# Head pairs 0 and 1 of a hybrid attention layer: attention weights as two 16-bit parts, turned by transposing transfers

## The chip, the cores and the metric

The kernel runs on one core of a Trainium2 chip. A core has TensorE (matrix products, results only into PSUM), VectorE (called DVE in the profile), ScalarE (ACT), GpSimd (POOL) and SyncE (SP, whose queue issues most transfers). Each engine works through its own queue in order; semaphores make one wait for another. The metric is the time of one launch in microseconds of device time. Three runs of the kernel before took 662.28, 662.69 and 664.75 us, so its median is 662.69 us.

## The reference

One layer on a sequence of 1024 positions, width 1024, all in float32:

```python
mod = silu(c) @ w_ada + b_ada                      # shift, scale, gate
u   = layer_norm(x) * (1 + scale) + shift
h   = u @ w_in                                     # q, k, v, g of both groups, and 8 forget gates
# stick-breaking heads (8):
z = q k^T / 8;  w = exp(log_sigmoid(z) + later)    # later: sum of log_sigmoid(-z) over the keys between
# forgetting heads (8):
p = softmax(q k^T / 8 + f_q - f_k), causal
y = concat(heads * silu(g)) @ w_out
out = layer_norm(2**0.25 * x + gate * y) * ln_g + ln_b
```

Heads are 64 wide. Two heads make a pair: pairs 0 to 3 are the stick-breaking heads, pairs 4 to 7 the forgetting ones. The change is in pairs 0 and 1.

## The kernel before

**Precision.** A float32 product is made of three products of rounded parts: both operands are split into a rounded part and a rest (`u_hi`, `u_lo`; `whi`, `wlo`), and hi x hi, lo x hi and hi x lo are added in PSUM (`m_step`, L329 to L331).

**Order.** The order of TensorE's instructions is written out by hand; the order on the other engines is made by a scheduler from the same text, and so is SP's after the start. In the first 80 us the input is normalised and turned (`u_turn`, `u_round`, `u_rest`), the first five projections are made (`start_steps`), and the value tiles of pairs 0 and 1 (`v_first`). Then come 128 units, one for a pair, a head and a block of 128 queries: `u = (p, h, i)`, `order(p)` gives their order. Around each unit TensorE gets a share of the remaining projections as filler (`fillers`, `FILL`: 52 steps around pair 0, 72 around pair 1, 68 around pairs 2 and 3). At the end comes the output projection (`o_step`, L1112 to L1114).

**A unit of pairs 0 to 3.** `att_scores` makes the scores in a PSUM tile S (L611, L613), ACT makes two sigmoids (`kp` at L646, `be` at L648), DVE a running product (L654, L658), POOL multiplies (L660): `be` now holds the unit's weights, 128 queries by (i+1) * 128 keys.

**From weights to output, pairs 0 and 1.** `att_transpose`, two units later (`LAG`), has TensorE turn each 128 x 128 block of `be` into a PSUM tile T (L691; two such tiles); ACT rounds it into `pt` (L693) and DVE subtracts for the rest (L694). Two units make a block of 256 queries; `att_pv` then multiplies both parts with the values in one 512-column product for each 128 keys (L720), and `att_sum` adds three pieces (L738 to L740), multiplies by the gate (L741) and stores.

**Pairs 2 and 3 (and 4 to 7) instead.** ACT writes `be` times 2**15 as float16 (L671), DVE the rest as float16 (L673), and SP issues a transposing transfer that turns both parts inside the SBUF tile called `home` (L572). `att_pv` comes five units later (`LAG_CROSSED`) and makes two float16 products of 256 columns for each 128 keys (L709). Values too are two float16 parts, scaled by a factor that `gen_ranges` finds beside the units of pair 0: sums of squares of the value weights (L396), the largest modulation (L386, L388), and from them a power (L408 to L422). `FIRST_CROSSED` is the first pair that goes this way.

PSUM is full: while T tiles are needed, S has one buffer; later the two banks of T become a second S.

## Time and profile before

| | |
|---|---|
| median of three runs | 662.69 us |
| the profiled execution | 664.71 us, its span 663.0 us |
| TensorE busy | 635.6 us (96%), weight loads 535.5 us |
| DVE, ACT, POOL busy | 511.8, 397.8, 344.3 us |
| first 80.2 us | projections and values of the start |
| pair 0, pair 1 (first to first weights) | 80.2 to 149.7, 149.7 to 223.6 us |
| pair 2, pair 3 | 223.6 to 287.9, 287.9 to about 345 us |

A line of the profile names the source line, the engine, the operation, output <- input, and the shape as partitions x elements; times are from the start of the span. A matmul's duration is from its start until its result is out, and neighbours overlap: what one adds to TensorE's queue is the distance from start to start. The stage boundaries are the starts of the first L648 of each pair.

### The profile page before, as it was taken

The page shows a single profiled execution, that of the slowest core. Times are in us where ns is not written, and L with a number is a line of the kernel's source. Part 1 is how long each engine was busy: PE and PEld are TensorE (multiplying, and loading weights), DVE is VectorE, ACT ScalarE, POOL GpSimd, SP SyncE. Part 2 cuts the span into 40 slices and gives each one's busy share as a digit, 9 for nine tenths or more (in the row PEclk, how much of TensorE's full clock was granted, in tenths as well). Part 3 has the DMA queues.
Part 4 walks back from the last instruction along what each step waited for, and adds up shares of the span by engine and source line. Part 5 has one row for each costly group of instructions (what it writes and reads, how often), then busy time and mean ns, then how long its engine had stood idle before and what let it go on. Part 6 is the DMA issues. An engine that isn't in the chain of part 4 may idle for free. (4 is left out here: it accounts for less than half of the span.)

```text
span 663.0 us, 10902 instructions
## 1 busy us (share of the span) xinstructions
PE 635.6 (96%) x3558; PEld 535.5 (81%) x3558; DVE 511.8 (77%) x1011; ACT 397.8 (60%) x833; POOL 344.3 (52%) x429
## 2 busy tenths in 40 slices
...
GB/s 319 402 312 135 167 123 110 104 58 28 58 33 10 71 115 112 160 118 157 106 172 153 174 139 153 139 147 125 115 198 137 245 284 176 205 232 129 94 33 63
DMA packets 153800, 96.25 MB, mean 145 GB/s; under 512 B 118224, under 2 KB 133136, under 8 KB 153744
## 3 DMA queue, kind: packets, MB, share of 16 engines
...
q14 instruction: 28, 0.23, 0.1%
...
## 5 line engine op out<-in xcount | busy, mean ns | idle before, releaser
L329 PE MATMUL m<-uh,whi 128*128 128x512 f32 x304 | 123.0, 405 | 1.2 <-DVE kl L316 1.2
L331 PE MATMUL m<-uh,wlo 128*128 128x512 f32 x304 | 119.8, 394 | 0.0
L330 PE MATMUL m<-ul,whi 128*128 128x512 f32 x304 | 119.8, 394 | 0.0
L660 POOL TENSOR_TENSOR be<-be,kp 128x127 f32<-128x127 f32 (+3 forms) x64 | 89.9, 1405 | 44.9 <-DVE kp L658 24.2
L741 POOL TENSOR_TENSOR ty<-ty,sg 64x256 f32<-64x256 f32 x64 | 49.8, 779 | 91.6 <-DVE ty L736 56.0
L654 DVE TENSOR_TENSOR_SCAN kp<-kp,floor 128x128 f32<-128x128 f32 (+3 forms) x64 | 58.5, 914 | 14.8 <-ACT kp L646 14.1
L611 PE MATMUL S<-k,q 128*128 128x512 f32 (+4 forms) x192 | 68.5, 358 | 1.0 <-ACT be L648 1.0
L331 PEld LDWEIGHTS m<-uh,wlo 128*128 128x128 f32 x304 | 57.2, 188 | 13.6
L329 PEld LDWEIGHTS m<-uh,whi 128*128 128x128 f32 x304 | 57.4, 189 | 12.0 <-PE m L331 1.2
L613 PE MATMUL S<-kl,qz 128*128 128x512 f32 (+4 forms) x192 | 65.8, 344 | 0.0
L330 PEld LDWEIGHTS m<-ul,whi 128*128 128x128 f32 x304 | 57.4, 189 | 9.7
L622 DVE CUSTOM_DVE_ANT_0 a<-S,fb 128x1024 f32<-128x1024 f32 (+7 forms) x64 | 48.2, 753 | 19.7 <-PE S L613 15.8
L628 ACT ACTIVATE a<-a,nm 128x1024 f32<-128x1024 f32 (+7 forms) x64 | 49.7, 776 | 19.8 <-DVE nm L622 18.9
L638 DVE SCALAR_TENSOR_TENSOR home<-a,l,home 128x1024 f16<-128x1024 f32 (+7 forms) x64 | 58.1, 907 | 3.5 <-ACT home L634 3.3
L634 ACT ACTIVATE home<-a,l 128x1024 f16<-128x1024 f32 (+7 forms) x64 | 49.3, 773 | 16.2 <-DVE l L630 9.0
L646 ACT ACTIVATE kp<-S 128x384 f32<-128x384 f32 (+4 forms) x96 | 43.7, 491 | 23.7 <-PE S L613 21.9
L709 PE MATMUL pv<-home,v_g 128*128 128x256 f16 x480 | 56.3, 265 | 0.7 <-DVE ty L736 0.7
L709 PEld LDWEIGHTS <-v_g 128*128 128x128 f16 x480 | 44.2, 99 | 15.1 <-issue 9.8
L441 PE MATMUL v<-whi_v,uh 128*128 128x256 f32 (+1 forms) x192 | 54.7, 285 | 0.0
L443 PE MATMUL v<-wlo_v,uh 128*128 128x256 f32 (+1 forms) x192 | 54.4, 283 | 0.0
L442 PE MATMUL v<-whi_v,ul 128*128 128x256 f32 (+1 forms) x192 | 54.1, 282 | 0.0
L1112 PE MATMUL o<-woh,whi_y 128*128 128x512 f32 (+1 forms) x119 | 47.4, 398 | 5.4 <-DVE sg L322 4.8
...
## 6 DMA issues: line engine op xcount, KB each, us to landing
...
```

The source lines that it names most:

```text
L329: nc.tensor.matmul(acc, hi[:, c], u_hi[kt][:, s], start=(kt == 0), stop=False)
L330: nc.tensor.matmul(acc, hi[:, c], u_lo[kt][:, s], start=False, stop=False)
L331: nc.tensor.matmul(acc, lo[:, c], u_hi[kt][:, s], start=False, stop=(kt == NB - 1))
L441: nc.tensor.matmul(acc[:, :n], u_hi[kt][:, ts_], hi[:, s], start=(kt == 0), stop=False)
L442: nc.tensor.matmul(acc[:, :n], u_lo[kt][:, ts_], hi[:, s], start=False, stop=False)
L443: nc.tensor.matmul(acc[:, :n], u_hi[kt][:, ts_], lo[:, s], start=False, stop=(kt == NB - 1))
L611: nc.tensor.matmul(S[:, s, :w], qst[p][h][:, qs], kst[p][h][:, ks], start=True, stop=False)
L613: nc.tensor.matmul(S[:, s, :w], z, klo[p][:, ks], start=False, stop=not masked)
L638: lows[:] = [nc.vector.scalar_tensor_tensor(lo, ab, l, hi, op0=ALU.mult, op1=ALU.subtract)]
L654: last_dve = nc.vector.tensor_tensor_scan(rv, rv, floor[:, :ke - lo], initial=0.0, op0=ALU.mult, op1=ALU.max)
L660: nc.gpsimd.tensor_tensor(be[:, :ke - 1], be[:, :ke - 1], kp[:, 1:ke], op=ALU.mult)
L709: nc.tensor.matmul(acc[:, q0:256], vt[p][:, kb, h * P:(h + 1) * P], pt[:, 2 * kb + x_, q0:], start=(kb == 0 and x_ == 0), stop=(kb == last ...
```

## The change

`FIRST_CROSSED` goes from 2 to 0: pairs 0 and 1 go the way of pairs 2 and 3. T tiles, L691, L693, L694 and L720 are gone; S has two buffers from the first unit on. The values of pairs 0 and 1 are stored as float16 parts as they are made (`v_first`, in the start), so their factor is needed there: `range_sums`, four squares, `range_top`, `range_inverse` and `range_scales` stand in the last rounds of `start_steps`. `gen_ranges` keeps the factors of groups 1 to 3. The gate's last step (`gen_gate`) moves from beside pair 0 to beside pair 4. The order of units in pairs 0 to 3 is another, and the places in `home` for pair 0 are given by `FIRST_HOMES`.

```diff
@@ -25,7 +25,7 @@
 MASKED = -1.0e30
 BIG = 3.0e38
 UP = 2.0 ** 15
-FIRST_CROSSED = 2
+FIRST_CROSSED = 0
 
 
 @with_exitstack
...
@@ -376,16 +375,47 @@
 
     v_up, v_down, v_two = {}, {}, {}
 
+    rng = bss_sb.rearrange("p k i -> p (k i)")[:, 4:]
+
+    def range_sums():
+        nc.gpsimd.tensor_copy(modc[:, 1, :], bss_sb[:, 1, :])
+        m2 = bss_sb[:, 0, :]
+        nc.vector.tensor_reduce(out=m2, in_=modc.rearrange("p k i -> p i k"), op=ALU.max,
+                                axis=mybir.AxisListType.X, apply_absolute_value=True)
+        return nc.vector.tensor_tensor(rng[:, 0:1], m2[:, 0:1], m2[:, 1:2], op=ALU.add)
+
+    def range_top(row):
+        nc.tensor.transpose(row, rng[:, 0:1], ident)
+        return nc.vector.tensor_reduce(out=rng[0:1, 1:2], in_=row, op=ALU.max, axis=mybir.AxisListType.X)
+
+    def range_inverse(top_ps):
+        nc.tensor.matmul(top_ps, ones[0:1, :].to_broadcast([1, P]), rng[0:1, 1:2], start=True, stop=True)
+        top = rng[:, 2:3]
+        nc.vector.tensor_scalar(top, top_ps, 1.0e-30, None, op0=ALU.max)
+        nc.vector.reciprocal(top, top)
+
+    def range_scales(norm_ps, fr, g0, n):
+        nc.tensor.matmul(norm_ps, ones.to_broadcast([P, P]), fr, start=True, stop=True)
+        up, down = rng[:, 3 + g0:3 + g0 + n], rng[:, 7 + g0:7 + g0 + n]
+        nc.vector.tensor_reduce(out=up, in_=norm_ps.rearrange("p (g h) -> p g h", h=4), op=ALU.add,
+                                axis=mybir.AxisListType.X)
+        nc.vector.tensor_scalar(up, up, 1.0e-30, None, op0=ALU.max)
+        nc.gpsimd.tensor_tensor(up, up, mhalf.to_broadcast([P, n]), op=ALU.pow)
+        nc.gpsimd.tensor_scalar(up, up, rng[:, 2:3], 900.0, op0=ALU.mult, op1=ALU.mult)
+        nc.vector.reciprocal(down, up)
+        nc.vector.tensor_scalar(down, down, 1.0 / UP, None, op0=ALU.mult)
+        for g in range(n):
+            v_up[g0 + g], v_down[g0 + g] = up[:, g:g + 1], down[:, g:g + 1]
+
+    def square(out, w, at):
+        return nc.vector.tensor_tensor_reduce(out=out, in0=w, in1=w, op0=ALU.mult, op1=ALU.add, scale=1.0,
+                                              scalar=0.0, accum_out=at)
+
     def gen_ranges():
 
 
         for _ in range(NORM_AT):
             yield
-        nc.gpsimd.tensor_copy(modc[:, 1, :], bss_sb[:, 1, :])
...
@@ -393,35 +423,10 @@
                 raw = raw_tile(f"n{g}_{h}")[:, :n]
                 nc.sync.dma_start(raw, w_vf[h] if g == 1 else w_v[g - 1, h])
                 at = 4 * g - 4 + h
-                nc.vector.tensor_tensor_reduce(out=raw, in0=raw, in1=raw, op0=ALU.mult, op1=ALU.add, scale=1.0,
-                                               scalar=0.0, accum_out=fr[:, at:at + 1])
+                square(raw, raw, fr[:, at:at + 1])
                 for _ in range(NORM_SPACE):
                     yield
...
+        range_scales(s_tile("ranges", 2)[:, 0, :12], fr, 1, 3)
...
@@ -447,10 +452,11 @@
             v5 = v_two[g][:, :, t].rearrange("p i (x c) -> p i x c", c=HD)
             a5 = acc[:, :256].rearrange("p (i x c) -> p i x c", i=2, c=HD)
             up = v_up[g][:, 0:1]
-            nc.scalar.activation(v5[:, :, 0::3, :], a5, AF.Copy, scale=up)
+            upper = nc.scalar.activation(v5[:, :, 0::3, :], a5, AF.Copy, scale=up)
             for i in range(2):
-                nc.vector.scalar_tensor_tensor(v5[:, i, 1:3, :], a5[:, i], up, v5[:, i, 0::3, :],
-                                               op0=ALU.mult, op1=ALU.subtract)
+                v_evacs.append(upper)
+                v_evacs.append(nc.vector.scalar_tensor_tensor(v5[:, i, 1:3, :], a5[:, i], up, v5[:, i, 0::3, :],
+                                                              op0=ALU.mult, op1=ALU.subtract))
         for i in range(0 if g in v_two else 2):
             v4 = vt[2 * g + i].rearrange("p t (x c) -> p t x c", c=HD)
             a4 = acc[:, i * P:(i + 1) * P].rearrange("p (x c) -> p x c", c=HD)
...
@@ -540,6 +546,7 @@
     homes, parts_at = {}, []
 
     HOMES = ((1, 12), (2, 0), (1, 0), (0, 0))
+    FIRST_HOMES = ((2, 0), (0, 8), (0, 0), (2, 8), (1, 0), (0, 0), (2, 0), (1, 0))
     LAST_HOMES = ((2, 0), (2, 4), (4, 0), (4, 8), (0, 0), (1, 0), (4, 0), (0, 0))
 
     def home(n):
...
@@ -560,14 +567,14 @@
 
     def two_parts(u):
 
-        two = place(parts_at, ((3, 0, 16), (2, 8, 16)), u[2] + 1)
+        two = place(parts_at, ((3, 0, 16), (2, 8, 16)) if k_of[u] > 19 else ((3, 0, 16),), u[2] + 1)
         return two.rearrange("p b (x c) -> p b x c", x=2)
 
     def cross(u, two):
         p, h, i = u
         j, qo = i // 2, (i % 2) * P
         if (p, h, j) not in st_pt:
-            m, a = (LAST_HOMES if p == NPAIR - 1 else HOMES)[j if p < NPAIR - 1 else 2 * j + h]
+            m, a = FIRST_HOMES[2 * j + h] if p == 0 else LAST_HOMES[2 * j + h] if p == NPAIR - 1 else HOMES[j]
             st_pt[p, h, j] = home(m)[:, a:a + 4 * j + 4, :]
         sent[:] = [nc.sync.dma_start(st_pt[p, h, j][:, :2 * i + 2, qo:qo + P],
                                      two.rearrange("p b x c -> p (b x c)"), transpose=True)]
...
@@ -604,7 +611,7 @@
         qs = slice(i * P, i * P + P)
         if p >= 4:
             f = fb[2 * (p - 4) + h]
-        S = s_tile(f"S_{p}_{h}_{i}", 1 if k_of[u] < 16 * FIRST_CROSSED + LAG else 2)
+        S = s_tile(f"S_{p}_{h}_{i}", 2)
         halves = range(ns) if p >= 4 else range(ns)[::-1]
         for s in halves:
             ks = slice(s * w, s * w + w)
...
@@ -883,9 +890,12 @@
         last = kb == NB - 1
         if last:
             start_steps(ALL[:2], acc0, kb)
+            range_top(xt_early[0:1, :P])
             for n in range(2):
                 evac_m(*START[n], 0, acc0[n])
             start_steps(ALL[2:], acc0, kb)
+            range_inverse(xt_early[:, P:P + 1])
+            range_scales(xt_early[:, 2 * P:2 * P + 4], cm[:, :4], 0, 1)
             break
         start_steps(ALL[:4], acc0, kb, parts=(0,))
         if kb == 0:
...
@@ -941,6 +951,11 @@
             with after(rest, aggr[0]):
                 norm_stats(6)
             make_v(0)
+            with after(rest):
+                range_sums()
+                for n in range(4):
+                    square(v_two[0].rearrange("p i t c -> p (i t c)").bitcast(BF16)[:, :512],
+                           v0_raw[n], cm[:, n:n + 1])
 
     wg = {}
 
...
@@ -970,15 +981,16 @@
             parts.append((hi, lo))
             for _ in range(4):
                 yield
+        b = att_tile("bg")
+        nc.sync.dma_start(b, b_gate.to_broadcast([P, D]))
+        for _ in range(8):
+            yield
+        gp = s_tile("gate_ps", 2)
         for h in range(2):
             s = slice(h * 512, h * 512 + 512)
-            gp = t_tile(f"gate_{h}")
-
             for i, part in enumerate(parts[h]):
-                nc.tensor.matmul(gp, half.to_broadcast([P, P]), part, start=(i == 0), stop=(i == 1))
-            nc.vector.scalar_tensor_tensor(gate[:, s], b[:, s], 0.5, gp, op0=ALU.mult, op1=ALU.add)
-            yield
-            yield
+                nc.tensor.matmul(gp[:, h, :], half.to_broadcast([P, P]), part, start=(i == 0), stop=(i == 1))
+            nc.vector.scalar_tensor_tensor(gate[:, s], b[:, s], 0.5, gp[:, h, :], op0=ALU.mult, op1=ALU.add)
 
     def late_round(kb):
         u_turn(kb, 512, 1024)
...
@@ -1207,11 +1219,12 @@
 
     fillers = chain([
         beside(chain([gen_rest(), gen_v(0, v0_w, range(4, NB)), gen_m(1, 2), gen_m(2, 0), gen_m(2, 1)]),
-               gen_gate(), gen_ranges()),
+               gen_ranges()),
         gen_v(1),
         beside(chain([gen_m(2, 2), gen_m(3, 0), gen_m(3, 1), gen_m(3, 2)]), gen_forget()),
         gen_m(4, 0), gen_m(4, 1), gen_v(2),
-        gen_m(4, 2), gen_m(5, 0), gen_m(5, 1), gen_m(5, 2),
+        beside(chain([gen_m(4, 2), gen_m(5, 0)]), gen_gate()),
+         gen_m(5, 1), gen_m(5, 2),
         gen_m(6, 0), gen_m(6, 1), gen_v(3), gen_m(6, 2), gen_m(7, 0), gen_m(7, 1),
         gen_last_g(7),
     ])
...
@@ -1223,7 +1236,7 @@
     OUT0 = 5
     TAIL = (2, 2, 2, 2, 2, 2, 4, 4, 4, 4, 8)
     G7 = 6
-    HELD = {4: (1, 1), 5: (0, 0), 6: (1, 0), 10: (0, 1)}
+    HELD = {4: (1, 1), 5: (0, 0), 6: (1, 0), 8: (0, 1)}
     FIRST_UNITS = 5
     LNLOAD = 7
     YFIRST = 4
...
@@ -1231,17 +1244,16 @@
     done = [0]
 
     def fill(want):
-        while done[0] < want:
+        while done[0] < want - 1.0e-6:
             done[0] += 1
             next(fillers, None)
 
     def order(p):
         if p == 0:
-            return [(p, h, i + d) for i in (0, 4) for h in range(2) for d in range(4)]
-        if p < FIRST_CROSSED:
-            return [(p, h, i) for h in range(2) for i in range(NB)]
+            return [(p, h, i + d) for h in range(2) for i in (0, 2) for d in range(2)] + [
+                (p, h, i + d) for i in (4, 6) for h in range(2) for d in range(2)]
         if p < 4:
-            return [(p, h, i + d) for h in range(2) for i in (6, 4, 2, 0) for d in range(2)]
+            return [(p, h, i + d) for h in range(2) for i in (6, 2, 4, 0) for d in range(2)]
         if p < NPAIR - 1:
             return [(p, h, i) for h in range(2) for i in reversed(range(NB))]
         return [(p, h, i + d) for i in (2, 0, 4, 6) for h in range(2) for d in range(2)]
```

What the scheduler makes of it is shown at three places. The first is TensorE at the end of the first projections, where `ul_141` is the last block of the input's rest. Before:

```order
L826 MATMUL st_g_152<-ul_141,hw_461 128x512
L826 MATMUL st_q_153<-ul_141,hw_461 128x512
L826 MATMUL st_k_154<-ul_141,whi_sth_404 128x512
L441 MATMUL st_late<-v_home,uh_126 128x256
L442 MATMUL st_late<-v_home,ul_134 128x256
```

and with the change, first six rows earlier and then at the same place (`xT_early` is a PSUM tile; `bss_sb` holds the sums, `cm` the four squares):

```order
L833 MATMUL st_q_150<-ul_141,hw_461 128x512
L833 MATMUL st_k_151<-ul_141,hw_461 128x512
L388 MATMUL xT_early<-ident,bss_sb 1x128
L830 MATMUL st_g_152<-uh_133,hw_461 128x512
L830 MATMUL st_q_153<-uh_133,hw_461 128x512
```

```order
L833 MATMUL st_q_153<-ul_141,hw_461 128x512
L833 MATMUL st_k_154<-ul_141,whi_sth_404 128x512
L392 MATMUL xT_early<-bss_sb,ones 128x1
L398 MATMUL xT_early<-cm,ones 128x4
L446 MATMUL st_late<-v_home,uh_126 128x256
```

Three small products now stand in TensorE's queue ahead of the value tiles; each reads what DVE has made. The second place is DVE's queue at the same time. Before (`ul_141` and what follows it):

```order
L293 TENSOR_TENSOR ul_141<-xT_early,uh_133 128x512
L219 BN_STATS st_a_472<-x_370 128x6 x2
L209 BN_AGGR mv_a_475<-st_a_472 128x2
L303 SCALAR_TENSOR_TENSOR q_0_258<-st_q_150,q_0_258 64x512
L316 TENSOR_TENSOR kl_262<-st_k_151,k_0_260 64x512
L219 BN_STATS st_a_481<-x_375 128x6 x2
L303 SCALAR_TENSOR_TENSOR q_1_259<-st_q_150,q_1_259 64x512
L316 TENSOR_TENSOR kl_262<-st_k_151,k_1_261 64x512
L209 BN_AGGR mv_a_484<-st_a_481 128x2
L219 BN_STATS st_a_513<-x_377 128x6 x2
```

and with the change, in two pieces that follow each other (L411 is a sum of squares into `cm`):

```order
L292 TENSOR_TENSOR ul_141<-xT_early,uh_133 128x512
L383 TENSOR_REDUCE bss_sb<-modc 128x2
L411 ISA v_g_521,cm<-raws_367 128x512
L411 ISA cm 128x1
L218 BN_STATS st_a_472<-x_370 128x6 x2
L385 TENSOR_TENSOR bss_sb<-bss_sb 128x1
L411 ISA v_g_521,cm<-raws_367 128x512
L411 ISA cm 128x1
L302 SCALAR_TENSOR_TENSOR q_0_258<-st_q_150,q_0_258 64x512
L315 TENSOR_TENSOR kl_262<-st_k_151,k_0_260 64x512
L208 BN_AGGR mv_a_475<-st_a_472 128x2
L389 TENSOR_REDUCE bss_sb<-xT_early 1x1
```

```order
L218 BN_STATS st_a_481<-x_375 128x6 x2
L411 ISA v_g_521,cm<-raws_372 128x512
L411 ISA cm 128x1
L302 SCALAR_TENSOR_TENSOR q_1_259<-st_q_150,q_1_259 64x512
L315 TENSOR_TENSOR kl_262<-st_k_151,k_1_261 64x512
L394 TENSOR_SCALAR bss_sb<-xT_early 128x1
L208 BN_AGGR mv_a_484<-st_a_481 128x2
L218 BN_STATS st_a_513<-x_377 128x6 x2
L411 ISA v_g_521,cm<-raws_372 128x512
L411 ISA cm 128x1
```

The four squares stand between the statistics of `x` and the evacuations of q and k; the fourth is behind all of these. The third place is DVE in the second half of pair 0. Before (`pt` is written from a T tile):

```order
L654 SCALAR_TENSOR_TENSOR kp_0_7_1382<-kp_0_7_1382,floor 128x512
L658 SCALAR_TENSOR_TENSOR kp_0_7_1382<-kp_0_7_1382,floor 128x512
L322 SCALAR_TENSOR_TENSOR sg_1304<-sg_1304,m_2_0_1305 128x512
L694 TENSOR_TENSOR pt_0_3_0_1406<-T_0_6_0_1407,pt_0_3_0_1406 128x4x128
L694 TENSOR_TENSOR pt_0_3_1_1421<-T_0_6_1_1422,pt_0_3_1_1421 128x3x128
```

and with the change:

```order
L661 SCALAR_TENSOR_TENSOR kp_0_7_1403<-kp_0_7_1403,floor 128x512
L411 ISA n_2_1654,modc<-n_2_1654 128x512
L411 ISA modc 128x1
L665 SCALAR_TENSOR_TENSOR kp_0_7_1403<-kp_0_7_1403,floor 128x512
L680 SCALAR_TENSOR_TENSOR home_952<-be_1_5_1330,home_952 128x6x128
```

For each unit the one or two reads of PSUM (L694) are replaced by one instruction that reads `be` and the upper part from SBUF (L680, before L673).

More of the change, by code (lines that the diff above doesn't have):

```diff
@@ L97, in tile_hybrid_layer @@
     FROW = 16
-    GATE = 20
     NORM_SPACE = 5
```

32 lines of the change are left out of this document (removed).

## The prediction

> **What bounds the kernel now.** I read the share of the engines first, then windows by stage, then the waits of TensorE.
>
> ```profile
> PE 635.6 (96%) x3558; PEld 535.5 (81%) x3558; DVE 511.8 (77%) x1011; ACT 397.8 (60%) x833; POOL 344.3 (52%) x429
> ```
>
> Windows (us, then busy time of PE, PEld, DVE, ACT, POOL; granted clock, DMA share, GB/s): the start; pair 0, its first part and its middle; pair 1.
>
> ```profile
> 40.00:80.00 40.00, 40.00 (x239) 34.82 (x238) 32.72 (x61) 25.18 (x47) 8.78 (x15) 1.00 0.56 187
> 80.20:149.70 69.50, 62.01 (x340) 53.41 (x339) 58.67 (x101) 42.70 (x104) 47.98 (x60) 0.93 0.35 94
> 80.20:92.00 11.80, 11.80 (x66) 10.04 (x64) 6.47 (x11) 5.42 (x15) 10.19 (x14) 1.00 0.33 80
> 92.00:139.00 47.00, 39.51 (x221) 34.63 (x220) 43.84 (x79) 29.25 (x71) 31.39 (x38) 0.89 0.38 106
> 149.70:223.60 73.90, 73.90 (x465) 66.42 (x464) 54.39 (x107) 45.51 (x107) 42.96 (x59) 1.00 0.16 40
> ```
>
> In the start, in pair 0's first 11.8 us and in pair 1 TensorE never rests: what delays it or lengthens its queue there costs time, what DVE does is free. Only the rest of pair 0 is otherwise: in its middle DVE works 43.84 of 47 us, TensorE 39.5 at a clock of 0.89. The longest waits of TensorE there end on DVE:
>
> ```profile
> PE T L691 <- DVE pt L694: 3.4, 1, 3.4
> ```
>
> So pair 0 gains what DVE is relieved of, and the rest what TensorE is.
>
> **1. The start: a wait is added.** TensorE's first value product (L441) started at 45.10, and three small products now stand before it; the last (L398) reads the fourth square. DVE's queue after the last rest (L293) sets when that is done. Its timeline, and its groups between 42.2 and 53.6 us (count | busy, mean ns | idle):
>
> ```profile
> 45.10 0.28 PE L441 MATMUL st_late<-v_home,uh 128*128 128x256 f32 x1
> ```
>
> ```profile
> 41.63 0.69 DVE L293 TENSOR_TENSOR ul<-xT_early,uh 128x512 fp32r<-128x512 f32 x1 [1.74 <-ACT xT_early L281]
> 42.24 1.28 DVE L219 BATCH_NORM_STATS2 st_a<-x 128x6 f32<-128x512 f32 x2
> ```
>
> ```profile
> L219 DVE BATCH_NORM_STATS2 st_a<-x 128x6 f32<-128x512 f32 x8 | 5.1, 668 | 0.0
> L303 DVE SCALAR_TENSOR_TENSOR q<-st_q,q 64x512 fp32r<-64x512 f32 x2 | 1.4, 688 | 0.1
> L316 DVE TENSOR_TENSOR kl<-st_k,k 64x512 fp32r<-64x512 f32 x2 | 1.4, 688 | 0.1
> L209 DVE BATCH_NORM_AGGREGATE mv_a<-st_a 128x2 f32<-128x12 f32 x4 | 0.8, 204 | 0.1
> ```
>
> The same sum of squares, in pair 0:
>
> ```profile
> L396 DVE CUSTOM_DVE_ANT_0 n<-n 128x512 f32<-128x512 f32 x4 | 2.9, 720 | 0.0
> ```
>
> By the order, from 42.24 to the end of the fourth square: four squares 2.9, six statistics 4.0, four evacuations of q and k 2.75, two aggregates 0.4, four tiny instructions at the aggregate's 0.2: 10.9 in all. The fourth square ends at 53.1, the value tiles start near 53.2 instead of 45.1: **+8.1** (7.5 where neighbours overlap, 8.8 where DVE must also wait for the evacuations' products). Nothing covers it: TensorE has no other work in its queue, and it was busy through the whole window above. Behind the waiting product stand the value tiles and then pair 0's scores; ACT and DVE, which split those values and feed the units, get them 8 us later too, and so does all that follows. DVE uses the gap for the statistics it has in its queue, but from 40 to 80 us it worked 32.7 of 40 without setting the end, so what it does early there shortens nothing.
>
> An idle TensorE also loses clock. In pair 0:
>
> ```profile
> 92.00:96.00 4.00, 1.76 (x12) 1.30 (x10) 3.97 (x8) 2.44 (x6) 1.32 (x3) 0.96 0.53 167
> 96.00:100.00 4.00, 3.78 (x21) 3.81 (x22) 3.91 (x8) 1.15 (x5) 3.17 (x6) 0.62 0.51 132
> 126.50:133.40 6.90, 6.17 (x21) 5.48 (x22) 6.03 (x9) 2.06 (x5) 4.39 (x5) 0.51 0.31 87
> ```
>
> After a stall the clock is near half for 3 to 7 us. After 8 us nearly idle I take 4 us of work lost at half rate: **+2.0** (1.5 to 3). The Trainium skill, "TensorE: Matmul & The Clock Gate", section "What's actually happening", has half rate follow a whole idle window of some 3.4 us, and full rate one busy window; by it this cost would be near 1.7. The trace differs in that 2.2 us of idleness in 4 were enough.
>
> **2. The gate's step moves** from DVE-bound pair 0 to pair 4, where TensorE is the bound: four products of 512 columns, at 1.85 / 8 = 0.23 each (the row for L720 below). **+0.9**; its DVE work is counted in part 3.
>
> **3. Pair 0, DVE.** What goes, and the nearest rows of what comes (groups of DVE in pair 0; of the whole span for L736 and L979; in pair 2, then pair 3, for L673):
>
> ```profile
> L694 DVE TENSOR_TENSOR pt<-T,pt 128x512 fp32r<-128x512 f32 (+3 forms) x21 | 11.0, 534 | 1.7 <-ACT pt L693 1.6
> L740 DVE TENSOR_TENSOR ty<-pv,ty 64x256 f32<-64x256 f32 x6 | 2.5, 417 | 0.1
> L739 DVE TENSOR_TENSOR ty<-pv,ty 64x256 f32<-64x256 f32 x6 | 2.5, 413 | 0.1
> ```
>
> ```profile
> L736 DVE SCALAR_TENSOR_TENSOR ty<-pv,bss_sb,ty 64x256 f32<-64x256 f32 x48 | 23.0, 480 | 12.1 <-ACT ty L735 10.7
> L979 DVE SCALAR_TENSOR_TENSOR gate<-bg,gate 128x512 f32<-128x512 f32 x2 | 1.3, 670 | 0.0
> ```
>
> ```profile
> L673 DVE SCALAR_TENSOR_TENSOR home<-be,home 128x896 f16<-128x896 f32 (+7 forms) x15 | 17.2, 1146 | 0.3 <-ACT home L671 0.2
> L673 DVE SCALAR_TENSOR_TENSOR home<-be,home 128x256 f16<-128x256 f32 (+7 forms) x16 | 14.7, 918 | 1.0 <-ACT home L671 0.8
> ```
>
> Out: 11.0 + 2.5 + 2.5 + 1.3 = 17.3. In: five L736 at 0.48 = 2.4, and L673 for 14 of the 16 units (the last two now fall into pair 1). One shape of it took 0.80 or 3.05:
>
> ```profile
> 272.25 3.05 DVE L673 SCALAR_TENSOR_TENSOR home<-be,home 128x640 f16<-128x640 f32 x1
> 302.43 0.80 DVE L673 SCALAR_TENSOR_TENSOR home<-be,home 128x640 f16<-128x640 f32 x1
> ```
>
> A pair has 9216 columns, these 14 units 7296: at the quiet rate 9.1 us, at pair 3's 11.6, at pair 2's some 15. I take 12.5, nearer pair 3, as POOL is busy 48 of 69.5 us here. Net: 17.3 - 2.4 - 12.5 = 2.4 less (5.8 less, or 0.1 more). DVE then works 56.3 us. Of its 10.8 idle before, 5.3 lie in the first 11.8 us, where TensorE is full: they stay, and of the rest I keep 2.5 (TensorE loses 64 turns and 32 products here and waits less; a second S lets scores run ahead). ACT only exchanges one rounding (L693) for another (L671) and has slack, 42.7 of 69.5 us; it is put at nothing. If it came late, L673 would wait; in pairs 2 and 3 that made 0.3 and 1.0 us of idle. 56.3 + 5.3 + 2.5 = 64.1 against 69.5: **-5.4** (-0.4 to -8.5).
>
> **4. Pair 1 and on, TensorE.** What is left of L691 and L720 after pair 0, in the windows of these lines, and from start to start in the timeline:
>
> ```profile
> 149.70:290.00 140.30, 12.14 (x80) 9.63 (x80) 1.00 0.35 77
> 149.70:290.00 140.30, 12.25 (x48) 8.42 (x48) 1.00 0.35 77
> ```
>
> ```profile
> 151.95 1.03 PE L691 MATMUL T<-ident,be 128*128 128x128 f32 x8
> 152.74 0.36 PE L611 MATMUL S<-k,q 128*128 128x256 f32 x1
> 138.76 2.00 PE L720 MATMUL pv<-pt,v 128*128 128x512 f32 x8
> 140.61 0.27 PE L691 MATMUL T<-ident,be 128*128 128x128 f32 x1
> 307.05 1.82 PE L709 MATMUL pv<-home,v_g 128*128 128x256 f16 x16
> 308.68 0.31 PE L611 MATMUL S<-k,q 128*128 128x128 f32 x1
> ```
>
> Out: 80 turns at 0.79 / 8 and 48 products at 1.85 / 8 make 19.0; by busy time it is 24.4. I take 19.9, near the distances. In: L709 at 1.63 / 16 = 0.10 for pair 1's 80 and the 44 that pair 0, five units late, leaves over: 12.4. So -7.5, if DVE keeps up. DVE in pair 1: 54.4, less L694,
>
> ```profile
> L694 DVE TENSOR_TENSOR pt<-T,pt 128x512 fp32r<-128x512 f32 (+3 forms) x26 | 13.8, 556 | 5.5 <-ACT pt L693 5.4
> ```
>
> and sixteen L739 and L740 (6.6), and with L673 as in pair 2 (17.2), eight L736 (3.8) and pair 0's last two units (2): 57 us of 66, or 86%. Two windows of pairs 2 and 3 stand about this:
>
> ```profile
> 256.60:287.90 31.30, 29.80 (x155) 24.01 (x155) 27.71 (x31) 22.49 (x48) 22.87 (x28) 1.00 0.65 138
> 287.90:318.00 30.10, 30.10 (x163) 24.77 (x163) 24.76 (x33) 22.75 (x50) 24.75 (x29) 1.00 0.66 131
> ```
>
> At 89% TensorE idled 1.5 of 31.3 us, at 82% never. Over a pair that is 0 to 3; I take 0.8. **-6.7** (-4.5 to -8.6).
>
> **Sum:** 8.1 + 2.0 + 0.9 - 5.4 - 6.7 = -1.1. The profiled execution took 664.71 us, 2.0 above the median; the sum is put on the median: 662.69 - 1.1 = **661.6**.
>
> **Rivals.**
> - *More relief than I take:* L673 runs at its quiet 0.80 per 640 columns (-8.5), pair 1 gains its full -8.6, the start costs 9.0; with the gate -7.2, so 655.5. For it: pair 3's row is nearer the quiet rate. Against: POOL is as busy here as beside the slow one.
> - *Slower: L673 is slowed by POOL.* Place: DVE in pairs 0 and 1. Steady L694 read PSUM, L673 reads two SBUF tiles, and 3.05 against 0.80 shows the price. Pair 0 gains 0.4, pair 1 4.5; with 10.1 + 0.9 that is +6.1: 668.8. It decides once L673 in pair 0 averages above about 1.05 us (15 / 14). The Trainium skill, "VectorE: DVE Perf Modes", section "Two Vector instructions with no wait between them", says that the second of two SBUF inputs comes through an interface that GpSimd shares; by it this rival is the forecast, and the trace agrees so far that the shape's time quadruples.
> - *The start wait costs nothing,* because DVE's work ahead is done during it and TensorE catches up: -11.2, 651.5. Against: TensorE was full from 40 to 80.
> - *SP's queue is late.* A transposing transfer holds SP for
>
> ```profile
> L572 SPq DMA_TRANSPOSE home<-home x96: 1169/1343/4202, 234.3 to 590.4; - x96
> ```
>
> (minimum, median, maximum ns), now amid pair 0's weight loads. If L709 waits for them, pair 0's 5.4 is lost: 667.0. Against: five units of lag are about 20 us.
>
> **How the numbers follow.** Forecast 0.44, more relief 0.20, slowed L673 0.24, free start 0.06, SP 0.06. The forecast's own range, from its terms' middle parts, is 656 to 666. The measurement tells 0.5% (3.3 us) from no change: 659.4 to 666.0. The forecast splits 0.15 faster, 0.27 same, 0.02 slower; relief and free start are faster; the slowed L673 is slower but for 0.04, SP slower by its 0.06. Faster 0.41, same 0.31, slower 0.28. The range reaches both main rivals: 651 to 669.
>
> **What would show it.** Right: TensorE idle about 8 us before the first value product, which starts near 53, then some us at half clock; DVE near 56 us in pair 0, which lasts about 64 us; pair 1 near 66 to 67 us with TensorE full; L673's successor (L680) near 0.9 us. Wrong: no gap near 45 to 53; pair 0 as long as before with L680 above 1.05 us; or TensorE waiting for `home`.

## The result, and the profile after

The change made the kernel slower. Four runs had a median of 674.43 us (673.02 to 676.71), against 663.02 for the kernel before beside them: the ratio is 1.0165, with a 95% interval of 1.0144 to 1.0187. The forecast was 661.6, the range 651 to 669. The profiled execution took 673.06 us, its span is 671.3.

The first table is read from the starts of the second sigmoid (L648 before, L655 after), first of each pair and last of pair 3:

| us | before | after | difference | forecast |
|---|---|---|---|---|
| first weights of pair 0 | 80.2 | 92.8 | +12.6 | +10.1 |
| pair 0 | 69.5 | 65.9 | -3.6 | -5.4 |
| pair 1 | 73.9 | 71.4 | -2.5 | -6.7 with all that follows |
| pairs 2 and 3, to the last sigmoid | 120.3 | 121.6 | +1.3 | |
| from there to the end of the span | 319.1 | 319.7 | +0.6 | gate +0.9 |

Windows of the profile after: the start, pair 0, pair 1, pair 2 (columns as in the prediction).

```profile
40.00:80.00 40.00, 33.11 (x187) 29.00 (x185) 27.08 (x58) 20.61 (x35) 11.39 (x17) 0.87 0.36 125
92.80:158.65 65.85, 56.68 (x312) 48.63 (x311) 57.78 (x85) 41.92 (x93) 44.42 (x53) 0.95 0.51 126
158.65:230.00 71.35, 63.76 (x421) 56.33 (x420) 62.05 (x88) 46.87 (x97) 48.18 (x58) 0.95 0.63 142
230.00:294.90 64.90, 61.20 (x315) 49.69 (x314) 52.47 (x63) 47.38 (x100) 50.83 (x61) 0.97 0.56 125
```

Pair 1, which TensorE filled before, now has 7.6 us in which TensorE stands, and a clock of 0.95. TensorE's longest waits over the whole span (us in total, times, longest):

```profile
PE pv L716 <- DVE ty L743: 12.0, 5, 6.0
PE o L1124 <- DVE sg L321: 4.7, 2, 3.5
PE v L446 <- DVE kl L315: 3.8, 2, 2.3
PE xT_early L398 <- DVE cm L411: 3.6, 1, 3.6
PE xT_early L388 <- DVE bss_sb L385: 3.3, 1, 3.3
PE S L618 <- ACT fscratch L523: 3.0, 1, 3.0
```

The wait for L321 stood in the kernel before too (4.8 us). L743 is DVE's reading of a finished product of values; until it has read, the one PSUM tile for these products is taken and the next L716 cannot start.

**The start.** TensorE's timeline after:

```profile
46.67 0.27 PE L388 MATMUL xT_early<-ident,bss_sb 128*1 128x128 f32 x1 [3.31 <-DVE bss_sb L385]
54.40 0.59 PE L398 MATMUL xT_early<-cm,ones 128*128 128x4 f32 x2 [3.58 <-DVE cm L411]
54.85 0.56 PE L446 MATMUL st_late<-v_home,uh 128*128 128x256 f32 x1
```

and DVE's, of which four rows matter:

```profile
42.52 1.73 DVE L411 CUSTOM_DVE_ANT_0 v_g<-raws 128x512 bf16<-128x512 f32 x1
...
45.38 1.24 DVE L385 TENSOR_TENSOR bss_sb<-bss_sb 128x1 f32<-128x1 f32 x1
46.54 0.68 DVE L411 CUSTOM_DVE_ANT_0 v_g<-raws 128x512 bf16<-128x512 f32 x1
...
53.66 0.67 DVE L411 CUSTOM_DVE_ANT_0 v_g<-raws 128x512 bf16<-128x512 f32 x1
```

The value tiles start at 54.85, not at the forecast 53.2: one square took 1.73 where its neighbours took 0.68, and an addition of one column 1.24. The fourth square so ends at 54.33 for 53.1, and L398 itself, put at 0.1, takes 0.45. Both long ones read two SBUF inputs (the square its weights twice) and began while GpSimd was in L887:

```profile
42.41 1.28 POOL L887 TENSOR_TENSOR v_home<-raws,v_home 128x512 fp32r<-128x512 f32 x1 [0.87 <-ACT v_home L886]
43.65 2.95 POOL L887 TENSOR_TENSOR v_w<-raws,v_w 128x512 fp32r<-128x512 f32 x2
```

The addition ends at 46.62, the last of these L887 at 46.60. The value tiles then run at half clock until 61. Four windows (columns as above):

```profile
47.38:50.79 3.41, 3.41 (x10) 2.21 (x8) 3.35 (x9) 1.67 (x4) 1.72 (x3) 0.50 0.10 22
50.79:54.21 3.42, 0.03 (x1) 0.00 (x0) 3.33 (x7) 1.24 (x1) 1.34 (x3) 1.00 0.99 335
54.21:57.62 3.41, 3.22 (x15) 3.22 (x16) 0.95 (x8) 0.00 (x0) 1.83 (x5) 0.50 0.76 292
57.62:61.03 3.41, 3.41 (x18) 3.41 (x18) 0.12 (x1) 0.63 (x2) 0.00 (x0) 0.50 0.03 11
```

The 12.6 us are 9.75 of delay and 2.85 more, for which half of some 6.2 us at half clock is enough. In these rows the clock changes at 47.38, 50.79, 54.21 and 61.03, that is, after 3.41 us or twice that, and it follows the stretch just ended: half after the idle one, and full after one in which TensorE worked from end to end. The Trainium skill ("TensorE: Matmul & The Clock Gate", section "What's actually happening") has full rate follow one busy window of some 3.4 us, in windows that run freely; the trace agrees, for the work began within a window (54.4), and full rate came at the end of the next.

**Pairs 0 and 1.** L680, the successor of L673, in pair 0 and in pair 1 (groups of DVE):

```profile
L680 DVE SCALAR_TENSOR_TENSOR home<-be,home 128x128 f16<-128x128 f32 (+7 forms) x14 | 15.8, 1128 | 0.0
L680 DVE SCALAR_TENSOR_TENSOR home<-be,home 128x1024 f16<-128x1024 f32 (+7 forms) x18 | 23.6, 1313 | 1.5 <-ACT home L678 1.4
```

The sum took 12.5 us for the first; it was 15.8. What makes single ones long is seen at 153, on DVE and on GpSimd:

```profile
153.04 4.71 DVE L680 SCALAR_TENSOR_TENSOR home<-be,home 128x896 f16<-128x896 f32 x1
...
158.28 1.22 DVE L680 SCALAR_TENSOR_TENSOR home<-be,home 128x1024 f16<-128x1024 f32 x1
```

```profile
152.82 0.73 POOL L748 TENSOR_TENSOR ty<-ty,sg 64x256 f32<-64x256 f32 x1
153.50 0.09 POOL L668 MEMSET be<- 128x1 f32 x1
153.55 1.29 POOL L144 TENSOR_TENSOR wlo<-raw,whi 128x512 fp32r<-128x512 f32 x1
154.81 2.00 POOL L667 TENSOR_TENSOR be<-be,kp 128x1023 f32<-128x1023 f32 x1
```

L680 began while GpSimd was in L748. GpSimd ran three more instructions back to back, to 156.81, and L680 ended 0.94 us after that: about the time in which one of 896 columns is done otherwise (1.06). The 1024 columns at 158.28, with GpSimd free, took 1.22. So L680 did not run slowly, it stood until GpSimd's chain was over. This is the prediction's rival of the slowed L673, in a harder form: a wait of 3.8 us here, not a lower speed.

It is no single case. Of the 31 L680 that begin between 92.8 and 230 us, 17 begin during a GpSimd instruction; two of these begin in its last 0.06 us and are not slowed, the other 15 take 0.2 to 3.6 us more than the quickest of their shape, 15.1 of 38.2 us together. Each of them ends, to within 0.02 us, its quickest time less 0.12 after the end of a GpSimd instruction. The 14 that begin with GpSimd free are quick. Thirteen of the 15 wait for the one instruction that is running; the one at 153 and one at 176 wait for more of them. GpSimd can be held in its turn:

```profile
168.27 2.55 DVE L680 SCALAR_TENSOR_TENSOR home<-be,home 128x1024 f16<-128x1024 f32 x1
```

```profile
167.74 2.00 POOL L667 TENSOR_TENSOR be<-be,kp 128x1023 f32<-128x1023 f32 x1
169.72 2.29 POOL L144 TENSOR_TENSOR wlo_v<-raw_v,whi_v 128x528 fp32r<-128x528 f32 x1
```

Here L680 goes on once L667 has ended (169.74), and the next, L144, takes 2.29 where some 1.3 is usual.

### The profile page after: what moved, and what is told of

Same layout as the page of the kernel before. It is cut to its first block, busy times and chain, and to the rows that moved or that the text cites. A ratio compares the mean times of both kernels' runs of the same rounds, so it can differ in the third digit from the quotient of the medians.

```text
span 671.3 us, 10804 instructions
## 1 busy us (share of the span) xinstructions
PE 626.3 (93%) x3496; PEld 525.6 (78%) x3496; DVE 528.8 (79%) x991; ACT 398.6 (59%) x809; POOL 355.6 (53%) x431
## 3 DMA queue, kind: packets, MB, share of 16 engines
q1 hardware_dynamic: 190048, 100.54, 61.2%
## 5 line engine op out<-in xcount | busy, mean ns | idle before, releaser
L667 POOL TENSOR_TENSOR be<-be,kp 128x127 f32<-128x127 f32 (+3 forms) x64 | 91.8, 1434 | 42.5 <-DVE kp L665 29.3
L748 POOL TENSOR_TENSOR ty<-ty,sg 64x256 f32<-64x256 f32 x64 | 53.5, 836 | 88.1 <-DVE ty L743 57.9
L716 PE MATMUL pv<-home,v_g 128*128 128x256 f16 (+1 forms) x640 | 76.4, 268 | 12.8 <-DVE ty L743 12.0
L716 PEld LDWEIGHTS <-v_g 128*128 128x128 f16 x640 | 59.5, 100 | 33.0 <-issue 18.2
L680 DVE SCALAR_TENSOR_TENSOR home<-be,home 128x128 f16<-128x128 f32 (+3 forms) x64 | 71.6, 1120 | 7.8 <-ACT home L678 7.4
L618 PE MATMUL S<-k,q 128*128 128x384 f32 (+4 forms) x192 | 68.1, 356 | 3.8 <-ACT fscratch L523 3.0
L661 DVE TENSOR_TENSOR_SCAN kp<-kp,floor 128x128 f32<-128x128 f32 (+3 forms) x64 | 58.6, 916 | 15.1 <-ACT kp L653 14.2
L620 PE MATMUL S<-kl,qz 128*128 128x384 f32 (+4 forms) x192 | 66.2, 346 | 0.0
L645 DVE SCALAR_TENSOR_TENSOR home<-a,l,home 128x1024 f16<-128x1024 f32 (+7 forms) x64 | 60.9, 951 | 3.7 <-ACT home L641 3.3
L678 ACT ACTIVATE home<-be 128x128 f16<-128x128 f32 (+3 forms) x64 | 43.8, 685 | 18.0 <-POOL be L667 10.2
```

Source lines behind the costliest of these rows:

```text
L618: nc.tensor.matmul(S[:, s, :w], qst[p][h][:, qs], kst[p][h][:, ks], start=True, stop=False)
L620: nc.tensor.matmul(S[:, s, :w], z, klo[p][:, ks], start=False, stop=not masked)
L645: lows[:] = [nc.vector.scalar_tensor_tensor(lo, ab, l, hi, op0=ALU.mult, op1=ALU.subtract)]
L661: last_dve = nc.vector.tensor_tensor_scan(rv, rv, floor[:, :ke - lo], initial=0.0, op0=ALU.mult, op1=ALU.max)
L667: nc.gpsimd.tensor_tensor(be[:, :ke - 1], be[:, :ke - 1], kp[:, 1:ke], op=ALU.mult)
L680: lows[:] = [nc.vector.scalar_tensor_tensor(lo, bb, UP, hi, op0=ALU.mult, op1=ALU.subtract)]
```

## The experiments

Each ratio is against the kernel before, run beside it; the last columns come from each run's profile, as in the first table. A profile shows one execution: that of e8 took 680.79 us, of e11 670.26 and of e13 661.03, where their medians are 676.24, 665.91 and 663.44.

| kernel | ratio (95%) | first weights | pair 0 | pair 1 | pair 2 |
|---|---|---|---|---|---|
| the change | 1.0165 (1.0144 to 1.0187) | 92.8 | 65.9 | 71.4 | 64.9 |
| e1 fixed scale | 1.0015 (1.0000 to 1.0029) | 79.8 | 65.2 | 75.1 | 64.9 |
| e2 small units first | 1.0201 (1.0186 to 1.0216) | 91.6 | 65.3 | 69.7 | 72.0 |
| e3 one SBUF input | 1.0048 (1.0031 to 1.0065) | 91.4 | 63.1 | 66.5 | 64.7 |
| e4 squares first | 1.0100 (1.0072 to 1.0129) | 89.1 | 65.8 | 71.4 | 64.8 |
| e5 chain first | 1.0151 (1.0126 to 1.0176) | 87.6 | 64.9 | 71.8 | 65.0 |
| e6 shared rest | 1.0259 (1.0227 to 1.0290) | 91.1 | 68.1 | 75.9 | 63.8 |
| e7 e5 and e6 | 1.0204 (1.0172 to 1.0236) | 87.6 | 70.3 | 73.4 | 62.3 |
| e8 gate back | 1.0207 (1.0168 to 1.0246) | 92.0 | 69.5 | 73.5 | 65.0 |
| e9 e1 and e3 | 0.9911 (0.9896 to 0.9926) | 79.8 | 63.3 | 68.1 | 65.0 |
| e10 exchanged | 1.0073 (1.0056 to 1.0090) | 91.1 | 66.2 | 69.7 | 61.2 |
| e11 e10 and e5 | 1.0045 (1.0016 to 1.0073) | 90.0 | 64.8 | 68.2 | 61.5 |
| e12 before, exchanged | 1.0004 (0.9990 to 1.0018) | 80.0 | 68.4 | 74.3 | 62.9 |
| e13 squares on ScalarE | 1.0007 (0.9981 to 1.0032) | 82.6 | 63.6 | 71.4 | 64.7 |
| e14 e10 and e13 | 0.9903 (0.9868 to 0.9939) | 82.7 | 67.0 | 67.9 | 61.2 |

**e1: no scale from data in the start.**

```diff
-            range_top(xt_early[0:1, :P])
...
-            range_inverse(xt_early[:, P:P + 1])
-            range_scales(xt_early[:, 2 * P:2 * P + 4], cm[:, :4], 0, 1)
...
+            nc.gpsimd.memset(v_up[0], 64.0)
+            nc.gpsimd.memset(v_down[0], 1.0 / 64.0 / UP)
```

> The scale of group 0 is a constant, 64: no squares, no sum and no small products in the start; sum, maximum and inverse for groups 1 to 3 are made beside pair 0 again. Left out: that the scale of group 0 follows the data. Theory S (the start's wait is carried to the end): the first weights start near 80.5 us instead of 92.8, and the time falls by 12 us, to about 662 (660 to 664). Rival (VectorE is the bound of pairs 0 and 1 anyway, and work that it does ahead in the gap is then missing): it falls by 6 to 8 only, to 666 to 668.

The first weights come 12.9 us earlier, and 0.0150 of the time goes, about 10 us. Theory S's mechanism holds (79.8 for its 80.5); the time, 665.61, lies between its number and the rival's: pair 1 took 75.1 us, 3.7 more, with the range's own waits now in it.

```profile
PE ranges L398 <- DVE bss_sb L394: 2.3, 1, 2.3
PE ranges L392 <- DVE bss_sb L389: 0.8, 1, 0.8
```

**e2: small units first in pair 1.**

```diff
+        if p == 1:
+            return [(p, h, i + d) for h in range(2) for i in (0, 2, 4, 6) for d in range(2)]
```

> Pair 1 takes its units in the order 0 to 7 for each head, not 6 7 2 3 4 5 0 1, so that two large units, not six in a row, stand between the ends of pair 0 and the small ones of pair 1. Theory O (VectorE piles up over six large units, which makes the 6.0 us wait of L716 near 160): the wait goes, and 6 to 8 us with its half clock, to 667 to 669. Rival V (VectorE has too much work in the pair wherever the units stand): the waits move, and the time stays within 2 us, 672 to 676.

Theory O falls: a wait of 5.0 us for L743 stays in pair 1, and pair 2 takes 72.0; the time, 677.68, is above both numbers. The run does not settle rival V, for the six large units now stand where pair 1 meets pair 2, and TensorE waits there for a transposing transfer:

```profile
247.55 3.36 PE L716 MATMUL pv<-home,v_g 128*128 128x256 f16 x16 [8.48 <-DMA home<-home]
```

**e3: no second SBUF input.**

```diff
+                        if p < 2:
+                            lows[:] = [nc.vector.tensor_scalar(lo, bb, 2.0 ** -40, 2.0 ** -40, ...)]
```

> For pairs 0 and 1 the rest of the weights (L680) is replaced by a VectorE instruction of the same size that reads only be; the rest is then nearly zero, so the lower parts of these weights are left out. Theory P (an instruction with two SBUF inputs waits until GpSimd's current instructions end): none of the replaced ones is above 1.25 us, their mean in pair 0 falls from 1.13 to about 0.7 or less, the waits of L716 for L743 fall from 11.3 to under 5 us, and the time by 6 to 9, to 665 to 668. Rival T (TensorE bounds these pairs, VectorE's waits are covered): less than 2 us. Rival N (VectorE is slow there for its own volume and not for the second input): the replaced ones are as long as L680, and the time stays.

1.17% goes, some 8 us. The replaced instructions, by line in pair 0 and in pair 1, and the two windows:

```profile
L681 DVE TENSOR_SCALAR home<-be 128x128 f16<-128x128 f32 (+7 forms) x14 | 9.8, 699 | 0.0
L681 DVE TENSOR_SCALAR home<-be 128x896 f16<-128x896 f32 (+7 forms) x17 | 13.5, 796 | 0.0
```

```profile
91.40:154.50 63.10, 52.72 (x292) 45.64 (x291) 53.41 (x83) 41.51 (x92) 37.00 (x50) 0.92 0.56 135
154.50:220.90 66.40, 66.11 (x441) 58.80 (x440) 55.20 (x90) 47.31 (x98) 45.99 (x61) 1.00 0.73 149
```

TensorE fills pair 1 again, at full clock, and pair 1 takes 66.5 us, where my count of products had given 73.9 - 7.5 = 66.4. So the count was right. Two parts of the expectation failed: the waits for L743 fell from 12.0 to 7.2 over the span, not under 5, and five of the 31 one-input instructions took over 1.25 us (the longest 1.71, again begun during a GpSimd instruction).

Which ones are held shows by their shape. At 384, 640 and 896 columns the new instruction takes as long as L680 (0.52, 0.79, 1.06 us); none of these twelve is slowed, though five begin during a GpSimd instruction. At 128, 256, 512, 768 and 1024 it is quicker by itself (1024: 0.67 for 1.22); all nine of these that begin during a GpSimd instruction are slowed. So one SBUF input alone does not decide it. And not all of the gain is the wait: for the same 31 units DVE's time falls from 38.2 to 23.3 us, of which 9.3 is less waiting and 5.7 the shorter instruction (by the quickest of each shape). Theory P holds for the larger part; how the 8 us divide between the two, this run does not show.

**e4 and e5: the queues reordered in the start.** In e4 the squares come first on DVE; in e5 the sum and the maximum before them, and the later statistics behind. Both put the small products among the value products:

```diff
+    next(first_tile)
+    next(first_tile)
+    range_inverse(xt_early[:, P:P + 1])
+    next(first_tile)
+    for _ in range(3):
+        next(third_tile)
+    range_scales(xt_early[:, 2 * P:2 * P + 4], cm[:, :4], 0, 1)
```

> The whole change, but the four squares and the sum stand ahead of the later statistics and of the evacuations of q and k on VectorE, and the three small products stand in TensorE's queue behind 18, 24 and 30 value products. Theory S: the fourth square ends near 49 to 50 us, TensorE idles 2 us or less, and the first weights start near 82 to 83; the time falls by 9 to 11, to 663.5 to 665.5. Rival (the evacuations of the value tiles wait for the scale anyway and TensorE waits for their PSUM): TensorE idles behind the second or third tile instead, and less than 6 us come back, 668 or more.

> As e4, but the chain itself comes first on VectorE: the sum and the row maximum ahead of the squares, and the statistics of the later rows of x and the evacuations of q and k behind them; the first small product stands among the first projections, where it stood, the second behind 12 and the third behind 36 value products. Theory S (the start's loss is the place of these instructions in two queues, and not their work): TensorE idles under 2 us between 43 and 62, the first weights start at 81.5 to 83.5, and the time is 664 to 667 on this chip. Rival (the statistics are now what is late: the turns of the second half of x wait): first weights at 86 or later, 668 or more.

e4 wins back 3.7 us of the start and 0.0065 of the time (4.3 us, not 9 to 11): TensorE now waited 4.3 us for the row maximum, which stood behind the squares; the rival's number came, for another reason than the one it gave. e5 wins back 5.1 of the start, and its rival was right: the second half of x is late.

```profile
PE xT L272 <- DVE x L237: 2.6, 2, 2.2
```

What e5 has ahead at the last sigmoid (5.7 us) is 1.8 at the end of its span, and under 1 by the ratios. After the last sigmoid TensorE idles 17.6 us in e5 and 15.1 in the change, 2.2 of the 17.6 a wait for `y7l` that the change does not have; the cause no run shows.

**e6 and e7: every second subtraction on GpSimd.**

```diff
+                        on = nc.gpsimd if p < 2 and u[2] % 2 else nc.vector
+                        lows[:] = [on.tensor_tensor(lo, bb, hi, op=ALU.subtract)]
```

> The factor 2**15 is put into the running product, so that L680 becomes a plain subtraction, and in pairs 0 and 1 every second unit's subtraction goes to GpSimd; the results are the same. VectorE loses some 20 us of work in the two pairs, GpSimd gains 25 to 30. Theory P (what hurts is VectorE held by GpSimd's instructions): TensorE waits less for L743, pairs 0 and 1 are 4 to 7 us shorter, 668 to 671. Rival G (GpSimd, at 46 of 66 and 48 of 71 us, becomes the late one, and its longer chains hold VectorE's other subtractions longer): 674 to 680.

> e5 and e6 together. If the start's term and the port's term are independent, the two gains add up: with theories S and P 658 to 662, below the kernel before. If pairs 0 and 1 are bound by the same engine as before, the sum is 3 us or more short of that.

Theory P's number failed, rival G's came (680.61, just above its end): GpSimd carries the longer chain, TensorE waits 11.7 us for transfers that start late, and DVE's remaining sixteen subtractions still take 1.25 us each:

```profile
L681 DVE TENSOR_TENSOR home<-be,home 128x128 f16<-128x128 f32 (+3 forms) x16 | 20.0, 1248 | 4.1 <-ACT home L678 4.1
```

```profile
PE pv L717 <- DMA home<-home: 11.7, 2, 7.2
```

e7 (677.65) is far from its 658 to 662: it is e6 less 0.0055, 3.6 us. With rival G in it, it says nothing on whether the two losses add up.

**e8: the gate's step back beside pair 0.**

```diff
-               gen_ranges()),
+               gen_gate(), gen_ranges()),
```

> The gate's last step stands beside pair 0 again, with its products in a PSUM tile of S. My term for its move was +0.9 on the time; if pair 0, bound by VectorE, takes it worse than pair 4, bound by TensorE, the time rises by 1 to 2 (675.5 to 677.5); if the term holds, it falls by about 1.

Its ratio is 0.4% above the change's, but the two intervals overlap. In its profile, the slowest of its four executions, pair 0 is 3.6 us longer, and TensorE waits 4.2 us there for the gate's own evacuation, which is in DVE's queue:

```profile
PE gate_ps L992 <- DVE gate L993: 4.2, 1, 4.2
```

So the move was probably a gain and not my +0.9; the times alone do not show it. The kernel before had a T tile for these products, so that this isn't its old cost.

**e9: e1 and e3 together.**

> e1 and e3 together: a constant scale for group 0 and no second SBUF input in the rests of pairs 0 and 1 (left out as there). If the loss is the start's term and the port's term, and the two are independent, the gains of 10 and 8 add up: 656 to 658, some 7 us below the kernel before, with pair 0 near 62, pair 1 near 69 (the range's products stand there now). If the two share a cause, the time is 661 or more.

0.0254 below the change: 16.8 us, where e1 and e3 alone gave 9.9 and 7.8. The two losses are separate and add up, to within 1 us. Without both, the change is 0.9% faster than the kernel before; but some of the work is left out with them.

**e10 and e12: VectorE and GpSimd exchange two steps.** The second sigmoid stays in PSUM, DVE multiplies there, GpSimd subtracts; the factor 2**15 is in the running product:

```diff
-            last_act = nc.scalar.activation(v3(be), S[:, :ns, :w], AF.Sigmoid)
+            last_act = nc.scalar.activation(S[:, :ns, :w], S[:, :ns, :w], AF.Sigmoid)
...
-            nc.gpsimd.tensor_tensor(be[:, :ke - 1], be[:, :ke - 1], kp[:, 1:ke], op=ALU.mult)
+                last_dve = nc.vector.tensor_tensor(be[:, a:b], S[:, s, :b - a], kp[:, a + 1:b + 1], op=ALU.mult)
...
+                    lows[:] = [nc.gpsimd.tensor_tensor(lo, bb, hi, op=ALU.subtract)]
```

> The whole change, but in pairs 0 to 3 VectorE and GpSimd exchange two steps: ScalarE leaves the second sigmoid in PSUM, VectorE multiplies it there with the running product (one PSUM and one SBUF input), and GpSimd subtracts the rounded part. The amount of work on both engines stays about the same; the results are the same. Theory P (VectorE loses time only by waiting with two SBUF inputs): no long instructions of VectorE are left in pairs 0 to 3, pair 1 is bound by TensorE, 66 to 67 us, pair 0 62 to 64, and the time falls by 7 to 10, to 665 to 668. Rival (S is now held until the multiplication, and its two buffers run out): TensorE waits for S instead, and less than 3 us come back.

> The kernel before (pairs 0 and 1 unchanged, start unchanged), with the exchange of e10 in pairs 2 and 3 alone, which go by transposing transfers there already. If VectorE's waits with two SBUF inputs cost TensorE time in pair 2 (1.5 us idle of 31.3, and 0 in pair 3), pair 2 falls from 64.3 to about 61.5 and the time by 2 to 3, to 661 to 662 (ratio 0.996). If S is short of buffers as in e10, nothing comes back.

e10 wins 0.9%, 6 us, less than expected. DVE's multiplication with one PSUM input, and TensorE's new wait:

```profile
L669 DVE TENSOR_TENSOR be<-S,kp 128x127 f32<-128x127 f32 (+5 forms) x96 | 50.4, 553 | 5.6
```

```profile
PE S L618 <- DVE be L669: 7.8, 5, 3.9
```

No multiplication was held by GpSimd: 64 of the 96 begin during one of its instructions, and those of one shape differ by 0.02 us at most. Pairs 1 and 2 gain 1.7 and 3.7, but pair 0 nothing: there the rival's shortage of S takes it (6.4 of the 7.8 us). e12, the same in pairs 2 and 3 of the kernel before, shortens pair 2 by 1.4 us and changes no time that can be measured.

**e11, e13, e14: what remains of the start.**

> e10 with the start of e5. If both theories hold and add up, 5 us less than e10: 660 to 663, level with the kernel before or below it.

e11 (median 665.91) is 3.5 us below e10, not 5, and does not reach its number. Its profile, of one of its slowest executions, has the first weights at 90.0 and two waits of TensorE for transfers (6.3 us); it does not show what the median lacks.

e13 is e5 with the squares on ScalarE:

```diff
-                    squares.append(square(..., v0_raw[n], cm[:, n:n + 1]))
+                    nc.scalar.activation(..., v0_raw[n], AF.Square, accum_out=cm[:, n:n + 1])
```

> e5 with the four squares on ScalarE (a square with an accumulated sum), which is 45 to 75% idle between 43 and 58 us; the results are the same. Theory W (what is left of the start's loss in e5, 7.5 of 12.6 us, is VectorE's amount of work there, with the squares that wait for GpSimd): the first weights start at 82 to 84 instead of 87.6, and the time falls by 4 to 5 below e5, to 667 to 669. Rival C (it is the chain of steps from the sum to the scale, which has the same hops): first weights at 86.5 or later, and less than 2 us.

> e13 with the exchange of e10, all of the reference's work in it. If W and P hold and add up: e11's time less 4 to 6, 660 to 662, that is 2 to 4 us below the kernel before; with C it stays at e11's 665 to 666.

Theory W holds for the start: the first weights come at 82.6, 10.2 us before the change's, and the chain from the sum to the scale is unchanged. More time goes than expected (663.44 us for 667 to 669), 0.0144 or some 9.5 us against e5; 5.0 of it lie in the start, the rest the runs do not explain. The engines in e13:

```profile
43.00:58.00 15.00, 13.34 (x102) 12.51 (x101) 11.26 (x30) 10.35 (x21) 7.62 (x15) 1.00 0.52 179
```

The clock stays at 1.00. The squares on ScalarE take 2.5 us and 0.8 for their sums:

```profile
L952 ACT ACTIVATE v_g<-raws 128x512 bf16<-128x512 f32 x4 | 2.5, 631 | 0.0
L952 ACT ACTIVATION_READ_ACCUMULATOR v_g<-raws 128x1 f32 x4 | 0.8, 192 | 0.0
```

e13 alone is level with the kernel before. e14, with the exchange too, does all of the reference's work in 658.79 us, a ratio of 0.9903 (0.9868 to 0.9939): it beats both kernels. That is a little below its expectation. Its pair 0 is still 67.0 us; whether more is to be had there was not tried.

## Why the prediction was wrong, by its own steps

**What bounds each stage: right for the start and pair 0.** The start followed TensorE, pair 0 DVE; in pair 1 TensorE no longer set the time alone. Between the sum's -1.1 and the profile's +8.4 lie 9.5 us: 2.5 in the start, 1.8 in pair 0, and 5.2 in pair 1 and what follows.

**Part 1, the start: mechanism right, size short.** The terms 8.1 + 2.0 came as 9.75 + 2.85; the first lies outside its bounds of 7.5 to 8.8. The step that failed is the use of quiet durations: the square at 0.72 and the tiny addition at 0.2 came as 1.73 and 1.24, once each. The row of the squares that I quoted was a mean; longer single ones, up to 1.69, were in the same trace and I left them out. e1 confirms that nothing covers the delay; e13, against e5, that 5.0 of the 7.5 us that e5 left of it hung on the squares on DVE.

**Part 2, the gate: too small, and the sign open.** In the change the four products take 2.4 us of TensorE's queue, from 369.40 to 371.83, 1.2 of it a wait for the evacuation L993, which the term did not have. Beside pair 0, in e8, they made TensorE wait 4.2 us on DVE.

**Part 3, pair 0: -3.6 for -5.4,** inside its bounds. L673's 12.5 should have been 15.8, above the bound of 15, and 6.3 of that is waiting for GpSimd; DVE worked 57.8 us for 56.3. With the input gone (e3) pair 0 took 63.1, which is no test of the sum's 64.1, as its instructions then took 9.8 and not 12.5.

**Part 4, pair 1: the main error.** The products were counted right (e3: TensorE works 66.1 of 66.4 us). The step that failed is the cost on DVE of the rests of the weights, and of its being late. For L673 I took pair 2's 17.2 us and 2 for pair 0's last two units, and L680 took 23.6; and I gave 0.8 us for DVE being late, read from two windows of pairs 2 and 3 by DVE's share of busy time. That share came as forecast, 62.05 us of 71.35 or 87%; yet one wait took 6.0 us, and half clock followed:

```profile
166.26 3.38 PE L716 MATMUL pv<-home,v_g 128*128 128x256 f16 x16 [6.04 <-DVE ty L743]
```

Sixteen products in 3.38 us where 1.8 is usual. What came late is L743, and what stood ahead of it on DVE is the L680 at 153.04 and one more:

```profile
162.50 2.05 DVE L680 SCALAR_TENSOR_TENSOR home<-be,home 128x896 f16<-128x896 f32 x1
165.71 0.49 DVE L743 SCALAR_TENSOR_TENSOR ty<-pv,bss_sb,ty 64x256 f32<-64x256 f32 x1
```

DVE is hardly idle between 153.04 and 165.71, and these two took 3.6 and 1.0 us more than the quickest of 896 columns: 4.6 of the 6.0. The busy share of a stage does not tell this: held instructions in a full queue are enough, when the next product needs a read that stands behind them. Pairs 0 and 1 together took 137.3 us, where the forecast, with all of its -6.7 put into pair 1, has 131.3; in e3 they took 129.6.

**What the sum did not have.** Pairs 2 and 3 and the rest lose 1.9 us together; in pair 2 a new wait of 3.0 us (L618 for `fscratch`) is in the list above. And the four runs' median lies 1.4 above the profiled execution, where that of before lay 2.0 below.

**The rivals.** The slowed L673 named the right cause, at 0.24; it gave 668.8 because it took the forecast's start and a loss of 3 us in pair 1, and it had the place wrong in part: pair 0 gained 3.6, not 0.4. Its point of decision, 1.05 us on average, was passed with 1.13. The Trainium skill's rule on the second SBUF input ("VectorE: DVE Perf Modes", section "Two Vector instructions with no wait between them") would have been the better guide: what e3 and e10 (none of 96 held) show agrees with it, and I gave it a quarter. SP's queue and the free start did not occur: L716 waited 0.9 us for a transfer in all. More relief did not occur either; e9 (0.9911, some 657 us) comes near its 655.5, but without the start's cost, which that rival kept.
